# A transformer layer with product-key experts: peer queries in float32, two more gather buffers, the dense sums converted in pairs

## The chip, the core and the metric

The kernel runs on one NeuronCore of one Trainium2 chip. The core has TensorE for matrix products (PE in the rows, PEld for its weight loads), VectorE (DVE), ScalarE (ACT), GpSimd (POOL) and SyncE (SP), which only issues transfers. All run their own instruction queues in order and meet through semaphores. Transfers between the chip's memory (HBM), SBUF and back run on 16 DMA engines; SP issues the plain ones, POOL the indirect ones (gathers). The metric is device time of one execution in microseconds, here 2284.3 (median of 3 runs, 2281.31 to 2289.24).

## What is computed

One layer on 256 tokens of width 2048, all in float32: a mixer (block attention and gated linear attention), cross attention to a memory of 256 tokens, and a product-key expert layer (PEER), each followed by a layer norm of ALPHA times the residual plus the result. The change touches the third part:

```python
q = (xt @ w_query).reshape(T, 8, 2, 128)              # 8 heads, 2 halves
s = einsum('thpd,hpnd->thpn', q, sub_keys)            # scores against 128 keys per half
s_top, i_top = top_k(s, 16)
cand = s_top[:, :, 0, :, None] + s_top[:, :, 1, None, :]
best, pos = top_k(cand.reshape(T, 8, 256), 16)        # 16 of 16384 experts per head
expert_idx, gates = ..., softmax(best)
h = gelu(einsum('td,thkd->thk', xc, expert_down[expert_idx]))   # rows of U
out = einsum('thk,thkd->td', gates * h, expert_up[expert_idx])  # rows of V
```

Each token has 128 slots (8 heads of 16), each slot one of 16384 experts, and each expert a row of 2048 floats in U (peer_u) and one in V (peer_v). A layer norm of ALPHA * x + out ends the kernel.

## The kernel before

The 256 tokens are two sets of 128, s = 0 and s = 1; 128 tokens are the 128 partitions of a tile.

**Split matmuls.** A float32 product is made of three faster ones in the type fp32r: an operand is split into a high part (`wh`, rounded by ACT, L151) and a low part (`wl`, the rest, by DVE, L152), and high x high, high x low and low x high are summed. The activations are split likewise: `h2` has its high part in columns 0 to 255 and its low part in columns 256 to 511 of each 128-row piece (L285, L286).

**Queries.** After the second layer norm (`ln_chunk`, four chunks of 512 columns for each token set) the queries of the heads are made: head 0 for token set 0 first (`scores_half`, L593), so that its route and the first gathers can start, with weights `pw` that are split in advance (`early`, and one piece on POOL); then head 1 for both sets (`peer_scores(1, 1)`), head 0 of set 1 (`scores_half` on raw weights), then heads 2 and 3, 4 and 5, 6 and 7 in pairs (`peer_scores(h0, 2)`), whose weights come in 1 MiB pieces through three buffers `wr`. With raw weights (`wl is None`, L206) PE multiplies in float32, once with the high and once with the low part of h2.

**Routes and gathers.** `route(s, h)` is some thirty small DVE instructions that end in `eidx`, the experts' numbers. `gather` (L671) issues on POOL one indirect transfer of 128 rows of 8 KB, 1 MiB, into the next buffer of a ring, and `u_row` (L685) multiplies it with the tokens on DVE and sums (L689, here called a row). The ring has the three buffers `g` of the pool gp, after head 0 of set 0 also the four slots of `gslots`, and for set 1 the three `wr` buffers (`gw`). All 128 slots of set 0 are gathered, of set 1 the first 83 (`KS = (128, 128 - S2)`). The program's order here is that of a scheduler, which moves instructions within its priorities.

**Dense part and last stage.** The sums over V of the slots gathered so far are not made by gathering: weights are written into matrices A[token, expert] (`one_hot`, `weigh_hot`, `build`; for set 0 in `aq0` and `aq1` during the gathers of set 1, for set 1 right after them in `a1` and in a spill in HBM), and `v_dense` (L804) multiplies A with all of V: 128 tiles of 128 experts, each one load of 1 MiB and 24 matmuls of 512 columns. In tile i ACT and DVE make high and low parts `ah`, `al` of the two 128 x 128 pieces of A (L820, L821; the elements lie 16 apart) and `wh`, `wl` of the tile of V. From here on the order is that of the code. Between the tiles `tick` runs a list of events (`deferred`): the other 45 slots of set 1 as rows of U, then as rows of V, which are added on DVE to `acc` (L697), ALPHA times the tokens of set 1. The events come at an even pace, 96 of them over 124 tiles; a row is gathered two events before DVE takes it. `finish` adds the sums of PE to the residuals and makes the last layer norm.

Of the kernel before, what the change touches and what calls it, by code (L numbers as in the profile page):

```python
# [16 lines left out]
P = 128  # L17
# [21 lines left out]
S2 = 45  # L39
# [17 lines left out]
class Body:  # L57
# [106 lines left out]
    def raw_tiles(self, w, c0):  # L164
        for g in range(4):
            yield g == 0, g == 3, g * 4, self.wload(w, c0, g), None
# [25 lines left out]
    def peer_q(self, xhl, tiles, dst, nc_):  # L192
        ps = [None] * (nc_ // T)
        for first, last, k0, wh, wl in tiles:
            for j in range(nc_ // P):
# [71 lines left out]
    def ln_chunk(self, y, stats, gb, dst, h, c):  # L267
# [15 lines left out]
        H = dst[:, 4 * c:4 * c + 4, h * P:(h + 1) * P]  # L283
        L = dst[:, 4 * c:4 * c + 4, T + h * P:T + (h + 1) * P]
# [285 lines left out]
    def pw_tiles(self, h, early=None, pool=()):  # L570
        for g in range(4):
            raw = self.pw[:, g * 4:(g + 1) * 4, h * T:(h + 1) * T]
            if g == 0 and early:
                wh, wl = early
            else:
                wh, wl = self.wsplit(raw, self.nc.gpsimd if g in pool else self.nc.vector)
            yield g == 0, g == 3, g * 4, wh, wl

    def pw_raw(self, h):
        for g in range(4):  # L580
            yield g == 0, g == 3, g * 4, self.pw[:, g * 4:(g + 1) * 4, h * T:(h + 1) * T], None
# [12 lines left out]
    def scores_half(self, s, h2, tiles):  # L594
        nc, ps = self.nc, self.bank()
        hs = slice(s * P, (s + 1) * P)
        for first, last, k0, wh, wl in tiles:
            n = wh.shape[1]
            for k in range(n):
# [256 lines left out]
    def run(self):  # L856
# [26 lines left out]
        with tc.tile_pool(name="smR", bufs=2) as self.sm:  # L883
# [13 lines left out]
            for c in range(4):  # L897
                self.ln_chunk(y, stats[0], gb, h2, 0, c)
# [128 lines left out]
```

## Time and profile before

| | |
|---|---|
| median of 3 runs | 2284.3 us |
| the profiled execution's own time | 2284.81 us |
| its span, first to last instruction | 2283.1 us |
| PE, PEld busy | 1830.5 us (80%), 1532.5 us (67%) |
| DVE, ACT, POOL busy | 1734.1 us (76%), 938.1 us (41%), 499.8 us (22%) |
| moved by DMA | 629.18 MB, mean 276 GB/s |

Busy shares over the whole span mix stages with different limits, so they are read by window: the stretch of a stage, the busy time of each engine in it, and the share of the 16 DMA engines (a little above 1 when all are full). In such a row the busy times stand in the order PE, PEld, DVE, ACT, POOL. Matmuls are pipelined, so that the mean of one is longer than the distance from one to the next.

### The profile page before, as it was taken

The page shows a single profiled execution, that of the slowest core. Times are in us where ns is not written, and L with a number is a line of the kernel's source. Part 1 is how long each engine was busy: PE and PEld are TensorE (multiplying, and loading weights), DVE is VectorE, ACT ScalarE, POOL GpSimd, SP SyncE. Part 2 cuts the span into 40 slices and gives each one's busy share as a digit, 9 for nine tenths or more (in the row PEclk, how much of TensorE's full clock was granted, in tenths as well). Part 3 has the DMA queues.
Part 4 walks back from the last instruction along what each step waited for, and adds up shares of the span by engine and source line. Part 5 has one row for each costly group of instructions (what it writes and reads, how often), then busy time and mean ns, then how long its engine had stood idle before and what let it go on. Part 6 is the DMA issues. An engine that isn't in the chain of part 4 may idle for free.

```text
span 2283.1 us, 24101 instructions
## 1 busy us (share of the span) xinstructions
PE 1830.5 (80%) x8702; PEld 1532.5 (67%) x8702; DVE 1734.1 (76%) x2517; ACT 938.1 (41%) x1546; POOL 499.8 (22%) x341
## 2 busy tenths in 40 slices
PE   8999999899999969994000550059999999999995
PEld 7778887788888858884000440047888888888884
DVE  5455556644444568899999999998888787888886
ACT  4554544444444441111210650056555555555553
POOL 0000000100000024766437337820111111111111
PEclk9999999999999989997555555579999999999998
DMA  7544557465546628999989999967889898999982
GB/s 229 173 161 155 163 181 276 139 193 186 198 134 221 228 89 329 412 422 379 344 301 364 338 311 347 394 240 270 332 339 347 323 366 314 357 360 330 342 346 92
DMA packets 159639, 629.18 MB, mean 276 GB/s; under 512 B 12176, under 2 KB 24592, under 8 KB 103840
## 3 DMA queue, kind: packets, MB, share of 16 engines
q1 hardware_dynamic: 116176, 312.01, 38.7%
q0 software_dynamic: 43344, 315.64, 36.7%
q8 instruction: 68, 1.11, 0.2%
q14 instruction: 51, 0.42, 0.0%
HBM read 620.27 MB, written 7.34 MB: 275 GB/s over the span
## 4 chain that ended last, share of the span: by engine, by line
PE 64%; DVE 23%; issue 5%; POOL 3%; DMA 3%; ACT 1%; ACTq 0%; SPq 0%; DVEq 0%; POOLq 0%
PE pp L183 9%; PE pp L831 6%; PE pp L830 6%; DVE g L689 6%; PE pp L833 6%; PE pp L224 5%; PE pp L225 5%; PE pp L223 5%; PE pp L185 5%; DVE gslots L689 5%; PE pa L830 4%; PE pa L831 4%; PE pa L833 4%; DVE oh L760 3%; DVE gw L689 2%
## 5 line engine op out<-in xcount | busy, mean ns | idle before, releaser
L152 DVE TENSOR_TENSOR wl<-wr,wh 128x1024 fp32r<-128x1024 f32 x512 | 627.9, 1228 | 418.5 <-ACT wh L151 418.2
L151 ACT CAST wh<-wr 128x1024 fp32r<-128x1024 f32 x512 | 538.4, 1052 | 556.4 <-PE pa L833 213.9
L689 DVE SCALAR_TENSOR_TENSOR g<-g,y 128x2048 f32<-128x2048 f32 x151 | 349.2, 2320 | 20.5 <-DMA g<-in_peer_u_dram,eidx 20.5
L680 POOL DMA_INDIRECT g<-in_peer_u_dram,eidx x151 | 232.9, 1542 | 494.3 <-DVE g L689 385.5
L830 PE MATMUL pp<-wh,ah 128*128 128x512 f32 x640 | 252.0, 394 | 2.3 <-issue 2.3
L831 PE MATMUL pp<-wl,ah 128*128 128x512 f32 x640 | 251.2, 392 | 0.9 <-DVE wl L152 0.7
L833 PE MATMUL pp<-wh,al 128*128 128x512 f32 x640 | 208.6, 391 | 0.0
L207 PE MATMUL pp<-h,wr 128*128 128x256 f32 x768 | 166.6, 379 | 0.0
L207 PEld LDWEIGHTS pp<-h,wr 128*128 128x128 f32 x768 | 145.7, 190 | 19.5
L830 PE MATMUL pa<-wh,ah 128*128 128x512 f32 x384 | 150.8, 393 | 0.0
L831 PE MATMUL pa<-wl,ah 128*128 128x512 f32 x384 | 150.4, 392 | 0.0
L689 DVE SCALAR_TENSOR_TENSOR gslots<-gslots,y 128x2048 f32<-128x2048 f32 x64 | 145.2, 2281 | 6.3 <-DMA gslots<-in_peer_u_dram,eidx 6.3
L736 PE MATMUL pa<-ident,w 128*128 128x128 f32 x2 | 0.9, 460 | 180.4 <-DVE w L705 180.4
L831 PEld LDWEIGHTS pp<-wl,ah 128*128 128x128 f32 x640 | 120.7, 189 | 28.5 <-DVE wl L152 2.6
L830 PEld LDWEIGHTS pp<-wh,ah 128*128 128x128 f32 x640 | 120.5, 188 | 27.9 <-issue 2.5
L833 PEld LDWEIGHTS pp<-wh,al 128*128 128x128 f32 x640 | 120.5, 188 | 27.3
L183 PE MATMUL pp<-x,wh 128*128 128x512 f32 x384 | 136.4, 398 | 0.0
L833 PE MATMUL pa<-wh,al 128*128 128x512 f32 x384 | 129.4, 391 | 0.0
L680 POOL DMA_INDIRECT gslots<-in_peer_u_dram,eidx x64 | 105.9, 1654 | 78.4 <-DVE gslots L689 46.7
L736 PEld LDWEIGHTS pa<-ident,w 128*128 128x128 f32 x2 | 0.4, 182 | 181.1 <-DVE w L705 166.2
L736 PE MATMUL pa<-ident,ij 128*128 128x128 f32 x4 | 1.3, 434 | 147.0 <-DVE ij L661 147.0
L820 ACT CAST ah<-aq 128x128 fp32r<-128x128 f32 x208 | 86.1, 414 | 73.6 <-PE pa L831 73.6
(310 smaller groups left out, 3759.2 us busy)
## 6 DMA issues: line engine op xcount, KB each, us to landing
wr<-in_peer_v_dram SPq DMA_DIRECT2D x128, 1024.0 KB, 6.4
wr<-in_w_in_dram SPq DMA_DIRECT2D x48, 1024.0 KB, 5.1
wr<-in_xattn_wkv_dram SPq DMA_DIRECT2D x32, 1024.0 KB, 5.2
wr<-in_w_out_dram SPq DMA_DIRECT2D x16, 1024.0 KB, 5.3
wr<-in_xattn_wq_dram SPq DMA_DIRECT2D x16, 1024.0 KB, 5.0
wr<-in_xattn_wo_dram SPq DMA_DIRECT2D x16, 1024.0 KB, 5.0
wr<-in_peer_wq_dram SPq DMA_DIRECT2D x12, 1024.0 KB, 15.7
spill<-stg SPq DMA_DIRECT2D x16, 320.0 KB, 2.8
```

Of the source, the lines that this page charges most:

```text
L151: self.nc.scalar.copy(wh, raw)
L152: (eng or self.nc.vector).tensor_tensor(wl, raw, wh.bitcast(F32), op=ALU.subtract)
L183: nc.tensor.matmul(ps[j], wh[:, k, c], xhl[:, k0 + k, :], start=(first and k == 0), stop=False, skip_group_check=True)
L185: nc.tensor.matmul(ps[j][:, :T], wl[:, k, c], xhl[:, k0 + k, 0:T], start=False, stop=(last and k == WK - 1), skip_group_check=True)
L207: self.nc.tensor.matmul(out, wh[:, k, c], x, start=start and i == 0, stop=stop and i == 1, skip_group_check=True)
L223: nc.tensor.matmul(ps[h], xh, wh[:, k, :], start=(first and k == 0), stop=False)
L224: nc.tensor.matmul(ps[h], xh, wl[:, k, :], start=False, stop=False)
L680: self.nc.gpsimd.indirect_dma_start(out=g, out_offset=None, in_=table, in_offset=bass.IndirectOffsetOnAxis(ap=self.eidx[:, s, i:i + 1], ax ...
L689: self.nc.vector.scalar_tensor_tensor(g, g, 1.0, self.h2n[:, s, :], op0=ALU.mult, op1=ALU.mult, accum_out=self.z[:, s, i:i + 1])
L830: nc.tensor.matmul(o, ah[th], wh[:, c, :], start=first, stop=False)
L831: nc.tensor.matmul(o, ah[th], wl[:, c, :], start=False, stop=False)
L833: nc.tensor.matmul(out[th][cp * WK + c], al[th], wh[:, c, :], start=False, stop=last)
```

## The change

Queries: h2 is kept once, unsplit, as the first half of a tile `h2s`, and all queries are float32 matmuls with raw weights, one where there were three of fp32r or two of float32. The splits of `pw` on ACT, DVE and POOL and the low half of h2 go. The other half of `h2s` is two slots of the gather ring: it has 5 buffers for head 0 of set 0 (3 before) and 9 after it (7 before); for set 1 it keeps 6. In the last stage the two pieces of A are converted for two tiles at once (`a_pair`, 256 columns, every second tile), the rows of V of set 1 are added in place to the tokens of set 1 in `h2n` (`acc` goes), which ACT scales by ALPHA after the last row of U, and S2 is 53 in place of 45: 75 slots of set 1 are gathered before the last stage and 53 in it, 114 events over 124 tiles.

```diff
-S2 = 45
+S2 = 53
...
-    def peer_q(self, xhl, tiles, dst, nc_):
+    def peer_q(self, xT, tiles, dst, nc_):
         ps = [None] * (nc_ // T)
-        for first, last, k0, wh, wl in tiles:
+        for first, last, k0, w in tiles:
...
-                out, c = ps[b][:, e * T:(e + 1) * T], slice(j * P, (j + 1) * P)
                 for k in range(4):
-                    start, stop = first and k == 0 and e == 0, last and k == 3
-                    if wl is not None:
-                        self.mm3(out, wh[:, k, c], wl[:, k, c], xhl, k0 + k, start, stop)
-                        continue
-                    for i in range(2):
-                        x = xhl[:, k0 + k, i * T:(i + 1) * T].bitcast(F32)
-                        self.nc.tensor.matmul(out, wh[:, k, c], x, start=start and i == 0, stop=stop and i == 1,
-                                              skip_group_check=True)
+                    self.nc.tensor.matmul(ps[b][:, e * T:(e + 1) * T], w[:, k, j * P:(j + 1) * P], xT[:, k0 + k, :],
+                                          start=first and k == 0 and e == 0, stop=last and k == 3,
+                                          skip_group_check=True)
...
-    def ln_chunk(self, y, stats, gb, dst, h, c):
+    def ln_chunk(self, y, stats, gb, dst, h, c, split=True):
...
+        if not split:
+            nc.scalar.copy(H, src)
+            return
...
-        for first, last, k0, wh, wl in tiles:
-            n = wh.shape[1]
-            for k in range(n):
-                xh, xl = h2[:, k0 + k, hs], h2[:, k0 + k, T + s * P:T + (s + 1) * P]
-                if wl is None:
-                    ops = [(xh.bitcast(F32), wh), (xl.bitcast(F32), wh)]
-                else:
-                    ops = [(xh, wh), (xh, wl), (xl, wh)]
-                for i, (x, w) in enumerate(ops):
-                    nc.tensor.matmul(ps[:, :T], x, w[:, k, :], start=first and k == 0 and i == 0,
-                                     stop=last and k == n - 1 and i == len(ops) - 1)
+        for first, last, k0, w in tiles:
+            for k in range(4):
+                nc.tensor.matmul(ps[:, :T], h2[:, k0 + k, s * P:(s + 1) * P], w[:, k, :], start=first and k == 0,
+                                 stop=last and k == 3)
...
         def add():
-            self.nc.vector.scalar_tensor_tensor(self.acc, g, self.w[:, s, i:i + 1], self.acc,
-                                                op0=ALU.mult, op1=ALU.add)
+            acc = self.h2n[:, s, :]
+            self.nc.vector.scalar_tensor_tensor(acc, g, self.w[:, s, i:i + 1], acc, op0=ALU.mult, op1=ALU.add)
...
+    def residual(self):
+        self.nc.scalar.activation(self.h2n[:, 1, :], self.h2n[:, 1, :], AF.Copy, scale=ALPHA)
...
+        ev.append(lambda: pend.append(self.residual))
         ev += [lambda i=i: row(self.v_row, i) for i in range(KS[1], SLOTS)]
...
+    def a_pair(self, n, r):
+        nc, ah, al = self.nc, [], []
+        for s in range(2):
+            src = self.a_slab(s, n)[:, :, r:r + 2].rearrange("p t i -> p i t")
+            ah.append(self.v.tile([P, 2, P], F32R, name=self.name("ah"), tag="ah", bufs=4))
+            al.append(self.v.tile([P, 2, P], F32R, name=self.name("al"), tag="al", bufs=4))
+            nc.scalar.copy(ah[s], src)
+            nc.vector.tensor_tensor(al[s], src, ah[s].bitcast(F32), op=ALU.subtract)
+        return ah, al
...
-            if i == 2:
-                nc.scalar.activation(self.acc, self.h2n[:, 1, :], AF.Copy, scale=ALPHA)
...
+            if i % 2 == 0:
+                ah2, al2 = self.a_pair(n, r)
+            ah, al = [t[:, i % 2, :] for t in ah2], [t[:, i % 2, :] for t in al2]
...
-            early = self.gp.tile([P, 2, 4, T], F32R, name="early", tag="g")
-            early = self.wsplit(self.pw[:, 0:4, 0:T], None, (early[:, 0], early[:, 1]))
...
-            h2 = self.hl_tile("h2")
+            h2s = self.hlp.tile([P, 4, D], F32, name="h2s", tag="hl")
+            h2 = h2s[:, 0:2, :].rearrange("p a (k t) -> p (a k) t", t=T)
...
-            self.slots = []
+            spare = [lambda k=k: h2s[:, k, :] for k in (2, 3)]
+            self.slots = spare
             self.gather_u(0, (0,))
-            self.slots = [lambda k=k: gs[:, k, :] for k in range(4)]
+            self.slots = spare + [lambda k=k: gs[:, k, :] for k in range(4)]
```

On DVE, between the indices of head 0 (eidx) and the first rows, the kernel before has these (pa is a transposed chunk of the tokens, g a gather buffer, y the tokens):

```order
L286 TENSOR_TENSOR h_6342<-pa_6519,h_6342 128x4x128
L152 TENSOR_TENSOR wl_6557<-pw,wh_6556 128x1024
L286 TENSOR_TENSOR h_6342<-pa_6529,h_6342 128x4x128
L286 TENSOR_TENSOR h_6342<-pa_6538,h_6342 128x4x128
L286 TENSOR_TENSOR h_6342<-pa_6548,h_6342 128x4x128
L152 TENSOR_TENSOR wl_6586<-pw,wh_6585 128x1024
L152 TENSOR_TENSOR wl_6614<-pw,wh_6613 128x1024
L152 TENSOR_TENSOR wl_6642<-pw,wh_6641 128x1024
L689 SCALAR_TENSOR_TENSOR g_6769,z<-g_6769,y 128x2048
L689 SCALAR_TENSOR_TENSOR g_6772,z<-g_6772,y 128x2048
L689 SCALAR_TENSOR_TENSOR g_6775,z<-g_6775,y 128x2048
L689 SCALAR_TENSOR_TENSOR g_6778,z<-g_6778,y 128x2048
```
and the changed kernel these, up to the first instruction of head 1's route (MAX):

```order
L271 TENSOR_TENSOR y<-y,ln_0_5733 128x512
L268 SCALAR_TENSOR_TENSOR y<-y,rr_6352,ln_1_5734 128x512
L669 SCALAR_TENSOR_TENSOR h2s,z<-h2s,y 128x2048 x2
L669 SCALAR_TENSOR_TENSOR g_6622,z<-g_6622,y 128x2048
L669 SCALAR_TENSOR_TENSOR g_6625,z<-g_6625,y 128x2048
L669 SCALAR_TENSOR_TENSOR g_6628,z<-g_6628,y 128x2048
L607 MAX val_6545<-sc_6538 128x8 x2
```
The four residuals of h2 and the four low parts wl are gone, and five rows stand where four stood.

On DVE, further on, between the indices of head 1 and the first MAX of head 2's route, the kernel before has 16 rows, of which these are the last 13 (w is the weights of head 0):

```order
L689 SCALAR_TENSOR_TENSOR g_6808,z<-g_6808,y 128x2048
L689 SCALAR_TENSOR_TENSOR g_6811,z<-g_6811,y 128x2048
L689 SCALAR_TENSOR_TENSOR g_6814,z<-g_6814,y 128x2048
L689 SCALAR_TENSOR_TENSOR gslots,z<-gslots,y 128x2048
L705 TENSOR_TENSOR w<-w,gate 128x16
L689 SCALAR_TENSOR_TENSOR gslots,z<-gslots,y 128x2048
L689 SCALAR_TENSOR_TENSOR g_7070,z<-g_7070,y 128x2048
L689 SCALAR_TENSOR_TENSOR g_7073,z<-g_7073,y 128x2048
L689 SCALAR_TENSOR_TENSOR g_7076,z<-g_7076,y 128x2048
L689 SCALAR_TENSOR_TENSOR gslots,z<-gslots,y 128x2048 x4
L689 SCALAR_TENSOR_TENSOR g_7087,z<-g_7087,y 128x2048
L627 MAX val_6980<-sc_6963 128x8 x2
```
and the changed kernel, from the indices on:

```order
L642 SCALAR_TENSOR_TENSOR eidx<-ij 128x16
L669 SCALAR_TENSOR_TENSOR g_6648,z<-g_6648,y 128x2048
L669 SCALAR_TENSOR_TENSOR g_6651,z<-g_6651,y 128x2048
L669 SCALAR_TENSOR_TENSOR g_6654,z<-g_6654,y 128x2048
L669 SCALAR_TENSOR_TENSOR h2s,z<-h2s,y 128x2048
L669 SCALAR_TENSOR_TENSOR g_6844,z<-g_6844,y 128x2048
L685 TENSOR_TENSOR w<-w,gate 128x16
L607 MAX val_6758<-sc_6741 128x8 x2
```
The route of head 2 stands behind 5 rows where it stood behind 16.

On DVE in the last stage the first three tiles of the kernel before read:

```order
L821 TENSOR_TENSOR al_9576<-aq_7941,ah_9575 128x128
L821 TENSOR_TENSOR al_9580<-a_9039,ah_9579 128x128
L152 TENSOR_TENSOR wl_9586<-wr_9021,wh_9585 128x1024
L152 TENSOR_TENSOR wl_9590<-wr_9021,wh_9589 128x1024
L821 TENSOR_TENSOR al_9621<-aq_7941,ah_9620 128x128
L821 TENSOR_TENSOR al_9625<-a_9039,ah_9624 128x128
L152 TENSOR_TENSOR wl_9631<-wr_9541,wh_9630 128x1024
L152 TENSOR_TENSOR wl_9635<-wr_9541,wh_9634 128x1024
L689 SCALAR_TENSOR_TENSOR g_9461,z<-g_9461,y 128x2048
L821 TENSOR_TENSOR al_9666<-aq_7941,ah_9665 128x128
L821 TENSOR_TENSOR al_9670<-a_9039,ah_9669 128x128
```
and two tiles and the start of the next of the changed kernel, a few tiles further on:

```order
L794 TENSOR_TENSOR al_9553<-aq_7581,ah_9552 128x256
L794 TENSOR_TENSOR al_9557<-a_8652,ah_9556 128x256
L152 TENSOR_TENSOR wl_9563<-wr_9478,wh_9562 128x1024
L152 TENSOR_TENSOR wl_9567<-wr_9478,wh_9566 128x1024
L669 SCALAR_TENSOR_TENSOR g_9513,z<-g_9513,y 128x2048
L152 TENSOR_TENSOR wl_9600<-wr_9515,wh_9599 128x1024
L152 TENSOR_TENSOR wl_9604<-wr_9515,wh_9603 128x1024
L669 SCALAR_TENSOR_TENSOR g_9550,z<-g_9550,y 128x2048
L794 TENSOR_TENSOR al_9635<-aq_7581,ah_9634 128x256
L794 TENSOR_TENSOR al_9639<-a_8652,ah_9638 128x256
```
The two al stand ahead of every second tile's wl, and are twice as wide.

## Rows read from the trace of the kernel before

**Rows 1.** page, part 2: busy tenths in 40 slices
```profile
DVE  5455556644444568899999999998888787888886
```
**Rows 2.** windows: length, busy (x) by engine, granted clock, DMA share, GB/s
```profile
846.00:860.00 14.00, 11.10 (x71) 9.96 (x72) 14.00 (x15) 3.40 (x5) 7.01 (x5) 0.73 0.57 201
860.00:900.00 40.00, 38.20 (x203) 33.96 (x203) 34.91 (x59) 4.54 (x12) 18.04 (x13) 1.00 0.80 291
900.00:1000.00 100.00, 100.00 (x480) 88.54 (x479) 84.72 (x131) 10.35 (x26) 75.98 (x35) 1.00 1.02 417
1000.00:1400.00 400.00, 123.50 (x517) 105.56 (x515) 399.25 (x775) 112.44 (x314) 183.23 (x134) 0.57 0.93 344
1400.00:1505.00 105.00, 0.66 (x2) 0.31 (x2) 93.67 (x91) 3.13 (x11) 90.24 (x40) 0.50 0.98 388
1505.00:1553.00 48.00, 38.02 (x258) 34.70 (x258) 44.94 (x150) 39.46 (x119) 0.41 (x1) 0.92 0.47 147
1553.00:2255.00 702.00, 701.06 (x3054) 574.35 (x3054) 582.45 (x648) 365.05 (x514) 98.83 (x87) 1.00 0.88 330
```
**Rows 3.** chain of waits, 812 to 862 us: start, us, what
```profile
819.51 1.12 DVE wl L152
...
821.24 1.61 DVE nmr L264
...
829.57 5.64 PE pp L606 x46
...
858.65 2.30 DVE g L689 x2
...
861.21 7.27 DMA g<-in_peer_u_dram,eidx
```
**Rows 4.** timelines, POOL and DVE: start, us, instruction, idle before
```profile
846.82 1.33 POOL L680 DMA_INDIRECT g<-in_peer_u_dram,eidx  x1 [18.90 <-DVE y L273]
...
868.58 2.29 DVE L689 SCALAR_TENSOR_TENSOR g<-g,y 128x2048 f32<-128x2048 f32 x1 [3.09 <-DMA g<-in_peer_u_dram,eidx]
```
**Rows 5.** groups by form, DVE, 850 to 1505 us: busy, mean, idle
```profile
L645 DVE TENSOR_TENSOR cand<-val 128x256 f32<-128x256 f32 x15 | 6.0, 403 | 0.0
L152 DVE TENSOR_TENSOR wl<-pw,wh 128x1024 fp32r<-128x1024 f32 x4 | 5.2, 1336 | 0.0
...
L286 DVE TENSOR_TENSOR h<-pa,h 128x512 fp32r<-128x512 f32 x4 | 2.6, 678 | 0.0
```
**Rows 6.** groups by form, DVE, 1400 to 1505 us
```profile
L689 DVE SCALAR_TENSOR_TENSOR g<-g,y 128x2048 f32<-128x2048 f32 x20 | 47.5, 2382 | 6.7 <-DMA g<-in_peer_u_dram,eidx 6.7
L689 DVE SCALAR_TENSOR_TENSOR gw<-gw,y 128x2048 f32<-128x2048 f32 x19 | 44.4, 2334 | 3.7 <-DMA gw<-in_peer_u_dram,eidx 2.8
```
**Rows 7.** groups by form, PE, 850 to 1505 us
```profile
L207 PE MATMUL pp<-h,wr 128*128 128x256 f32 x768 | 166.6, 379 | 0.0
```
**Rows 8.** timeline, ACT: score copies of two pairs of heads
```profile
938.38 1.72 ACT L592 COPY sc<-pa 128x256 f32<-128x256 f32 x4
...
995.47 1.72 ACT L592 COPY sc<-pa 128x256 f32<-128x256 f32 x4
```
**Rows 9.** tile wr, 850 to 1062 us: its loads, queue to landing
```profile
DMA to landing us min/median/max: 6.0/15.8/17.3
```
**Rows 10.** groups by form, DVE, 1580 to 2240 us
```profile
L697 DVE SCALAR_TENSOR_TENSOR acc<-g,w,acc 128x2048 f32<-128x2048 f32 x45 | 105.6, 2346 | 0.0
...
L821 DVE TENSOR_TENSOR al<-aq,ah 128x128 fp32r<-128x128 f32 x198 | 69.1, 373 | 4.7 <-ACT ah L820 2.4 <-PE pa L833 2.3
```
**Rows 11.** waits, 1580 to 2240 us: total, times, longest
```profile
PEld pp L831 <- DVE wl L152: 1.5, 3, 0.5
```
**Rows 12.** timelines, DVE and PE, one tile of the last stage
```profile
1915.76 1.22 DVE L152 TENSOR_TENSOR wl<-wr,wh 128x1024 fp32r<-128x1024 f32 x1
...
1918.97 0.39 PE L831 MATMUL pp<-wl,ah 128*128 128x512 f32 x1
```
**Rows 13.** windows of 5.5 us in the last stage
```profile
2199.50:2205.00 5.50, 5.50 (x26) 4.51 (x25) 5.20 (x6) 2.85 (x5) 1.07 (x1) 1.00 1.02 429
```

More of the change, by code (lines that the diff above doesn't have):

```diff
@@ L165, in raw_tiles @@
         for g in range(4):
-            yield g == 0, g == 3, g * 4, self.wload(w, c0, g), None
+            yield g == 0, g == 3, g * 4, self.wload(w, c0, g)
     def mm3(self, out, wh, wl, xhl, kt, first, last):
@@ L568, in prefetch, with pw_tiles @@
                 g * 512:(g + 1) * 512, 0:512].rearrange("(k p) c -> p k c", p=P))
-    def pw_tiles(self, h, early=None, pool=()):
+    def pw_tiles(self, h):
         for g in range(4):
-            raw = self.pw[:, g * 4:(g + 1) * 4, h * T:(h + 1) * T]
-            if g == 0 and early:
-                wh, wl = early
-            else:
[L576 to L581, printed above, removed]
+            yield g == 0, g == 3, g * 4, self.pw[:, g * 4:(g + 1) * 4, h * T:(h + 1) * T]
     def scores(self, s, h, lhs):
@@ L810, in v_dense @@
                 nc.sync.dma_start(self.a_slab(1, n + NB - 1)[:, t, :], self.spill[:, n - 1, t, :])
-            if i == 2:
-                nc.scalar.activation(self.acc, self.h2n[:, 1, :], AF.Copy, scale=ALPHA)
             if i == NK - 10:
                 self.ln3_vectors()
-            ah, al = [None] * 2, [None] * 2
-            for s in range(2):
-                src = self.a_slab(s, n)[:, :, r]
-                ah[s] = self.v.tile([P, P], F32R, name=self.name("ah"), tag="ah", bufs=4)
-                al[s] = self.v.tile([P, P], F32R, name=self.name("al"), tag="al", bufs=4)
-                nc.scalar.copy(ah[s], src)
-                nc.vector.tensor_tensor(al[s], src, ah[s].bitcast(F32), op=ALU.subtract)
+            if i % 2 == 0:
+                ah2, al2 = self.a_pair(n, r)
+            ah, al = [t[:, i % 2, :] for t in ah2], [t[:, i % 2, :] for t in al2]
             self.load_v(i + WR - 1)
@@ L894, in run @@
             sk = self.sk_transpose(sk, "pp")
-            h2 = self.hl_tile("h2")
+            h2s = self.hlp.tile([P, 4, D], F32, name="h2s", tag="hl")
+            h2 = h2s[:, 0:2, :].rearrange("p a (k t) -> p (a k) t", t=T)
             stats = [self.ln_finish(st, h) for h in range(2)]
             for c in range(4):
-                self.ln_chunk(y, stats[0], gb, h2, 0, c)
-            scored = self.scores_half(0, h2, self.pw_tiles(0, early, (3,)))
+                self.ln_chunk(y, stats[0], gb, h2, 0, c, split=False)
+            scored = self.scores_half(0, h2, self.pw_tiles(0))
             self.table(AF.Exp)
@@ L949, in run @@
             self.total_ticks = HB * WA + (NK - VE) * WV
-            self.acc = self.v.tile([P, D], F32, name="acc")
             self.a1 = self.v.tile([P, NB, P, IB], F32, name="a1")
@@ L967, in finish @@
         st = self.tiny.tile([P, 2, 4, 6], F32, name="st3", tag="bnst", bufs=2)
-        acc, mv, r, nmr = (self.h2n[:, 0, :], self.acc), [None] * 2, [None] * 2, [None] * 2
+        acc, mv, r, nmr = (self.h2n[:, 0, :], self.h2n[:, 1, :]), [None] * 2, [None] * 2, [None] * 2
         def chunk(h, c, engines):
```

6 lines of the change are left out of this document (2 added, 4 removed).

## The prediction

> **What bounds the kernel now.** I read the page's slices first, then the windows cut at the stages, then the chain of waits and the groups inside each window. In the slices VectorE (DVE) is at 8 to 9 tenths from the middle of the run to its end [rows 1]; the windows split that into stages with different limits (their busy columns are PE, PEld, DVE, ACT, POOL) [rows 2].
>
> From 846 to 1505 us lies the gather stage: 211 gathers of U, each 1 MiB, each followed by one dot product on DVE. DVE is busy 399.25 of the 400 us from 1000 to 1400: there it is the bound, with the DMA engines at 0.93. Before that it isn't: from 860 to 900 it works 34.91 of 40 us, from 900 to 1000 84.72 of 100, and the DMA engines are at 0.80 and 1.02 [rows 2]. So 5.1 + 15.3 = 20.4 us of DVE time are lost at the front. From 1400 to 1505 DVE works 93.67 of 105 us at 388 GB/s, and its idle time ends on gathers [rows 2, 6]: a tail of plain rows, bound by DMA.
>
> From 1553 to 2255 us lies the last stage, the 128 dense tiles of V. PE is busy 701.06 of 702 us, so it is the bound; DVE has 582.45 us of work there and the queues move 330 GB/s [rows 2]. The weight load waited for DVE 1.5 us in all, 3 times [rows 11]. Work put on DVE or the DMA engines here is free as long as the low part wl arrives before its matmul. In a tile with a row it is ready at 1915.76 + 1.22 = 1916.98 and used at 1918.97: 2.0 us of room [rows 12].
>
> **The change, part by part.** The sums go against the profiled execution (2284.8 us, span 2283.1); the median of the runs shown is 2284.3, so half a microsecond separates them.
>
> *Up to the first eidx.* The low part of a weight tile goes from DVE (1.12 us on the chain) [rows 3], and POOL's piece of the same split with it; behind it nmr, which writes one number per partition, took 1.61 us [rows 3], and I put 1.5 of that on the POOL op that ran beside it (an estimate; nothing else on DVE grew there). Together -2.6. The 46 matmuls that took 5.64 us [rows 3] become 14 behind the last transpose, in float32. Their price: 480 records fill 100 us of PE [rows 2], and each float32 matmul leaves two (768 records [rows 7] for 3 x 128 matmuls), so 0.417 us each and 5.8 for 14: no gain and no loss. PE has stood idle before them, and after such a pause its granted clock is 0.73 over 846 to 860 [rows 2]; wholly at the half level the 14 take 11.7, +6. Value -2.6, between -5 and +3.5.
>
> *From eidx to the first rows.* Four low parts (5.2 us) and four residuals of h2 (2.6 us) leave DVE [rows 5]: -7.8. They stand between eidx and the first row, where DVE never idles (14.00 of 14.00) [rows 2]. What is late next is the first gather: POOL issues it at 846.82 [rows 4], a gather took 7.27 us on the chain [rows 3], so no row can run before 854.1 where one now starts at 858.65 [rows 3]. DVE is ready 7.8 earlier, at 850.9, and waits 3.2. I keep -7.8 here and put that wait into the next term.
>
> *Idle of DVE at the front.* Five slots in place of three let gathers 4 and 5 go without waiting for a row; now row 4 waits 3.09 for its data [rows 4]. Then the scores: a pair of heads follows the one before by 995.47 - 938.38 = 57.1 us [rows 8], 53.3 of it float32 matmuls (256 records at 0.208). Half of these go, which leaves 30.4. Four loads of weights per pair through three buffers with 15.8 us to landing [rows 9] give (15.8 + 6.7) / 3 = 7.5 each, 30 a pair, so loads and matmuls are level. I put the scores of heads 2, 4 and 6 at some 907, 941 and 973, where now they stand at 938, 995 and 57 later. Routing is then there to fill DVE while gathers are late, and after head 1's indices the order has 5 rows ahead of it, not 16. Of the 20.4 I leave 12: 3 for the first gather, some 6 for rows 2 to 5 at the DMA pace, 3 for the first scores. Value -8, between 0 and -17 (all but the first wait).
>
> *Eight rows less.* At DVE's own price 8 x 2.36 = 18.9 [rows 6]; at the tail's pace, 105 us for 39 rows [rows 2, 6], 21.5. They go at the tail, so -20.
>
> *The last stage.* DVE gains 16 row instructions of 2.35 us [rows 10], 37.6 us. An al takes 373 ns for 128 elements [rows 10], now one of 256 replaces two. Nothing shows it; two of the old are 746, a contiguous one of 256 takes 403 [rows 5]. The row nearest in form is the strided al itself, so I take its slope above the fixed part: 403 ns for 256 contiguous elements against 678 for 512 [rows 5] is 1.07 ns an element over 128 fixed; (373 - 128) / 128 = 1.9 ns; 128 + 256 x 1.9 = 620. So 128 x 0.126 = 16 us are saved, and DVE stands at 582 + 22 = 604 of 702. By the contiguous row DVE would have 28 us less still; as PE is the bound, the sum stays. In tiles that make a pair DVE does up to 0.75 us more ahead of wl, out of 2.0 us of room; where two rows fall in one tile (four times, three before) PE may wait some tenths each. DMA: 16 MiB more, (330 x 702 us = 231.7 MB) + 16.8 = 248.4 MB, 354 GB/s, where 5.5 us windows reach 429 [rows 13]. The copy of the residual on ACT moves from tile 2 to the middle, into ACT's idle half. Value +1, between 0 and +6.
>
> Sum: -2.6 - 7.8 - 8 - 20 + 1 = -37.4, so 2284.8 - 37.4 = **2247.4**.
>
> **Rivals.** *The front is bound by bytes.* DMA is at 1.02 from 900 to 1000 [rows 2], and the weight loads come sooner, into the gathers. Then neither the shorter DVE list nor the earlier scores move the end, and only the tail and the first scores count: 2284.8 - 2.6 - 20 + 1 = 2263. For it: 417 GB/s there. Against: 860 to 900 runs at 291 GB/s [rows 2], 40 x 0.126 = 5 MB of room, five rows, which five slots can use. 0.2.
>
> *The last stage becomes bound by DMA* (the other side). A row that is late holds the wl queued behind it on DVE, and PE waits. The stage needs 248.4 MB; if the mix could give no more than the 330 GB/s it moved [rows 2], it would take 753 us, +51, and the total is 2298. It turns slower than before once the stage's rate falls under 248.4 MB / (702 + 37) us = 336 GB/s. For it: share 0.88 already. Against: 417 GB/s over 100 us, and 429 in this very stage [rows 2, 13]. 0.04 for slower, and 0.04 for a stage that gives the gain back and no more. The Trainium skill ("SBUF — State Buffer", section "Summary: rules for kernel authors") has transfers from HBM estimated at about 358 GB/s. By that figure the 2 MiB of a tile with a row need an estimated 5.86 us where a tile has 5.48, and a stage without slack would come out up to 40 us longer, at an estimated 2287; the windows at 417 and 429 [rows 2, 13] say that it is no ceiling on this core.
>
> *DVE in the last stage.* With al at 746 and two rows in a tile, PE waits up to 1.5 us four times, +6: 2252. It stays inside the forecast's range.
>
> *The spare slots don't serve*, because the gathers into h2's tile wait for the matmuls that read it. Then the first rows wait for the scores of head 1 and more, +30 on the front: 2277. Against: the matmuls read the first two quarters of that tile, the gathers fill the other two. 0.02.
>
> **How the numbers follow.** The forecast has 0.70, the byte-bound front 0.2, the dead slots 0.02, a last stage bound by DMA 0.04 near the old time and 0.04 slower. Ends: all terms at their low ends, -5 - 7.8 - 17 - 21.5 = 2234; at their high ends, the first wait not hidden, +3.5 - 4.6 - 18.9 + 6 = 2271. Range 2235 to 2266: it holds the forecast and the first rival, and leaves 0.15 to 0.2 out. Under 0.3% (7 us) this measurement tells nothing apart; the first three cases lie beyond it: faster 0.92, same 0.04, slower 0.04.
>
> **What would show it.** Right: score copies 57 apart now some 30 apart; first row within 4 us of its gather's landing and no L152 ahead of it; DVE from 860 to 1000 above 0.92 busy; a gather stage from eidx to the last gathered row of some 623 us, not 659; a last stage of 702 to 705 us with PE above 0.99 and windows of 350 GB/s; al of 256 at 0.5 to 0.7 us. Wrong: PE waiting for wl in the last stage by more than 6 us, or a front where DVE's idle of 20 us stays with the DMA engines at 1.0.

## The result, and the profile after

The changed kernel takes 2261.8 us (median of 4 runs, 2258.2 to 2266.6), the kernel before in the same session 2284.4: 22.6 us less. The ratio of the runs is 0.9892 (95% interval 0.9878 to 0.9907; the quotient of the two medians, 0.9901, lies in it). The profiled execution of the changed kernel is its fastest run, 2258.2 us with a span of 2256.5, and stands 26.6 us under the profiled one of before.

Cut at four points (the end of the first `eidx`, the end of the last gathered row, the start of the first dense matmul, the end of the last one), the two traces compare so, in us:

| stretch | before | changed | difference | put at |
|---|---|---|---|---|
| up to the first eidx | 845.9 | 844.1 | -1.8 | -2.6 |
| eidx to the last gathered row | 658.7 | 629.6 | -29.1 | -35.8 |
| to the first dense matmul | 48.0 | 48.9 | +0.9 | } |
| the dense tiles | 706.9 | 709.6 | +2.7 | } +1 |
| the last layer norm | 23.6 | 24.3 | +0.7 | } |

These are the four instructions in the timelines of the changed kernel (start, length, instruction):

```profile
843.95 0.18 DVE L642 SCALAR_TENSOR_TENSOR eidx<-ij 128x16 int32<-128x16 f32 x1
...
1471.45 2.29 DVE L669 SCALAR_TENSOR_TENSOR g<-g,y 128x2048 f32<-128x2048 f32 x1 [1.76 <-DMA g<-in_peer_u_dram,eidx]
...
1522.63 0.47 PE L818 MATMUL pp<-wh,ah 128*128 128x512 f32 x1 [2.77 <-issue]
...
2231.61 0.62 PE L821 MATMUL pa<-wh,al 128*128 128x512 f32 x2
```

The largest miss is the gather stage, 6.7 us longer than forecast; the stretches behind it are 3.3 us longer, the first one 0.8. The windows by stage (columns as in [rows 2]) say where the gather stage lost it:

```profile
846.00:860.00 14.00, 13.13 (x59) 11.23 (x60) 9.13 (x9) 2.30 (x4) 11.06 (x9) 0.82 0.75 270
860.00:900.00 40.00, 38.10 (x184) 33.20 (x183) 36.78 (x60) 3.66 (x12) 15.56 (x12) 1.00 1.01 406
900.00:1000.00 100.00, 71.87 (x319) 60.90 (x317) 85.92 (x194) 17.36 (x44) 45.05 (x33) 0.87 0.99 407
1000.00:1400.00 400.00, 68.66 (x259) 57.83 (x259) 399.30 (x719) 104.59 (x296) 188.96 (x136) 0.50 0.93 339
1550.00:2230.00 680.00, 677.26 (x2955) 554.56 (x2954) 581.81 (x528) 328.69 (x373) 143.30 (x100) 1.00 0.92 352
```

Against [rows 2]: VectorE has less to do right after the indices (9.13 us of 14, where it was full), and from 860 to 900 the DMA engines are now full. But from 900 to 1000 VectorE is still idle 14.1 us. Over 846 to 1000 its idle time is 154 - 131.8 = 22.2 us, where it was 20.4 and should have come to 12. In the kernel before, that idle time was waits on gathers (waits of VectorE from 846 to 1000 us: total, times, longest):

```profile
DVE g L689 <- DMA g<-in_peer_u_dram,eidx: 13.7, 11, 5.1
DVE gslots L689 <- DMA gslots<-in_peer_u_dram,eidx: 6.3, 9, 1.4
```

The same waits in the changed kernel name a piece that the prediction does not have:

```profile
DVE gr L649 <- ACT gate L647: 10.6, 1, 10.6
DVE g L669 <- DMA g<-in_peer_u_dram,eidx: 6.8, 4, 3.5
DVE h2s L669 <- DMA h2s<-in_peer_u_dram,eidx: 4.5, 2, 2.8
```

The gather waits are 11.3 us. The rest is one stall of 10.6 us in which VectorE waits for no gather at all, but for a tiny instruction of ScalarE in a route. The timeline of VectorE around it (start, length, instruction, idle time before it and what ended that):

```profile
977.27 0.41 DVE L613 FIND_INDEX8 pos<-best,mr 128x8 uint32<-128x256 f32 x1
988.28 0.16 DVE L649 RECIPROCAL gr<-gs 128x1 f32<-128x1 f32 x1 [10.61 <-ACT gate L647]
```

that of ScalarE:

```profile
982.29 0.59 ACT L204 COPY pq<-pp 128x512 f32<-128x512 f32 x1 [19.88 <-PE pp L200]
982.78 0.22 ACT L634 CAST idf<-idx 128x32 f32<-128x32 uint32 x1
985.75 0.59 ACT L204 COPY pq<-pp 128x512 f32<-128x512 f32 x1 [2.75 <-PE pp L200]
986.23 1.72 ACT L580 COPY sc<-pa 128x256 f32<-128x256 f32 x4
987.85 0.31 ACT L647 ACTIVATE gate<-best,gm 128x16 f32<-128x16 f32 x1
```

and that of TensorE:

```profile
978.54 7.17 PE L200 MATMUL pp<-h2s,wr 128*128 128x256 f32 x32 [2.64 <-DMA wr<-in_peer_wq_dram]
```

Read them from the last one: TensorE starts the last weight tile of heads 6 and 7 when it lands, at 978.5. ScalarE, in order, has been standing at the copy of those queries (`pq`) for 19.9 us. Behind that copy in its queue stands `gate`, whose input VectorE had written at 975, and for `gate` waits the reciprocal on VectorE, behind which stand rows that then run without a wait. In the chain of waits (start, us, what) the tile is the longest piece:

```profile
950.44 28.05 DMA wr<-in_peer_wq_dram
```

28 us for 1 MiB, where the loads of the kernel before landed after 6 to 17.3 us [rows 9].

### The profile page after: what moved, and what is told of

It is laid out like the page before. It is cut to its first block, busy times and chain, and to the rows that moved or that the text cites. A ratio compares the mean times of both kernels' runs of the same rounds, so it can differ in the third digit from the quotient of the medians.

```text
span 2256.5 us, 22663 instructions
## 1 busy us (share of the span) xinstructions
PE 1748.3 (77%) x8238; PEld 1454.3 (64%) x8238; DVE 1717.4 (76%) x2382; ACT 905.0 (40%) x1408; POOL 493.4 (22%) x348
## 3 DMA queue, kind: packets, MB, share of 16 engines
q8 instruction: 64, 1.05, 0.2%
## 4 chain that ended last, share of the span: by engine, by line
PE 68%; DVE 20%; DMA 6%; issue 4%; POOL 2%; ACT 1%; SPq 0%; ACTq 0%; DVEq 0%; POOLq 0%
PE pp L183 9%; PE pp L819 6%; PE pp L821 6%; PE pp L818 6%; PE pp L218 6%; PE pp L219 6%; PE pp L217 5%; PE pp L185 5%; DVE g L669 5%; PE pa L821 4%; PE pa L819 4%; PE pa L818 4%; DMA wr<-in_peer_wq_dram 3%; DVE oh L744 3%; DVE gslots L669 3%
## 5 line engine op out<-in xcount | busy, mean ns | idle before, releaser
L669 DVE SCALAR_TENSOR_TENSOR g<-g,y 128x2048 f32<-128x2048 f32 x138 | 316.6, 2304 | 12.2 <-DMA g<-in_peer_u_dram,eidx 12.2
L660 POOL DMA_INDIRECT g<-in_peer_u_dram,eidx x138 | 208.9, 1514 | 425.7 <-DVE g L669 343.6
L660 POOL DMA_INDIRECT g<-in_peer_v_dram,eidx x53 | 72.7, 1372 | 263.9 <-DVE y L678 235.0
L678 DVE SCALAR_TENSOR_TENSOR y<-g,w,y 128x2048 f32<-128x2048 f32 x53 | 124.4, 2347 | 0.0
L669 DVE SCALAR_TENSOR_TENSOR gslots<-gslots,y 128x2048 f32<-128x2048 f32 x48 | 109.7, 2301 | 0.0
L185 PE MATMUL pp<-x,wl 128*128 128x256 f32 x384 | 108.5, 283 | 0.0
L200 PE MATMUL pp<-h2s,wr 128*128 128x256 f32 x384 | 92.0, 401 | 17.6 <-DMA wr<-in_peer_wq_dram 17.6
```

Source lines behind the costliest of these rows:

```text
L185: nc.tensor.matmul(ps[j][:, :T], wl[:, k, c], xhl[:, k0 + k, 0:T], start=False, stop=(last and k == WK - 1), skip_group_check=True)
L660: self.nc.gpsimd.indirect_dma_start(out=g, out_offset=None, in_=table, in_offset=bass.IndirectOffsetOnAxis(ap=self.eidx[:, s, i:i + 1], ax ...
L669: self.nc.vector.scalar_tensor_tensor(g, g, 1.0, self.h2n[:, s, :], op0=ALU.mult, op1=ALU.mult, accum_out=self.z[:, s, i:i + 1])
L678: self.nc.vector.scalar_tensor_tensor(acc, g, self.w[:, s, i:i + 1], acc, op0=ALU.mult, op1=ALU.add)
```

## The experiments

Each was run beside the kernel before, on one chip and in one session; the ratio is to that.

| run | median, us | ratio | 95% interval |
|---|---|---|---|
| changed kernel | 2261.8 | 0.9892 | 0.9878 to 0.9907 |
| e1 copies behind | 2255.1 | 0.9870 | 0.9850 to 0.9891 |
| e2 no late weights | 2248.7 | 0.9839 | 0.9820 to 0.9859 |
| e3 45 slots | 2280.8 | 0.9988 | 0.9973 to 1.0002 |
| e4 old queries | 2269.3 | 0.9934 | 0.9917 to 0.9951 |
| e5 e1 with late vectors | 2249.3 | 0.9847 | 0.9833 to 0.9860 |
| e6 e5 with 61 slots | 2231.4 | 0.9770 | 0.9757 to 0.9783 |
| e7 no spare slots | 2267.1 | 0.9921 | 0.9908 to 0.9934 |
| e8 single pieces | 2256.9 | 0.9880 | 0.9865 to 0.9895 |
| e9 e5 with 65 slots | 2228.2 | 0.9755 | 0.9740 to 0.9770 |
| e10 e5 with 69 slots | 2244.1 | 0.9816 | 0.9802 to 0.9830 |
| e11 e6 with an early tile | 2229.0 | 0.9750 | 0.9736 to 0.9764 |
| e12 changed, late vectors | 2261.6 | 0.9898 | 0.9883 to 0.9913 |

**e1: is the stall a matter of order?** `gated` and `cast` are the last scaling of the gate and the cast `abf` of the route before; only ScalarE's order changes.

```diff
-                self.peer_scores(h0, 2, h2)
+                if h0 == 6:
+                    with tc.issue_after(self.gated.ins), tc.issue_after(self.cast.ins):
+                        self.peer_scores(h0, 2, h2)
+                else:
+                    self.peer_scores(h0, 2, h2)
```

> The changed kernel (2261.8 us), with one thing moved: on ScalarE the copies of the queries of heads 6 and 7 (pq, and the score copies behind them) stand behind the cast abf, the two gate instructions and the cast idf of head 5's route, and no longer ahead of them. Nothing else is reordered on any engine. In the trace of the changed kernel VectorE stands still for 10.6 us at 977.7, waiting for that gate, which stands behind the copies, which wait for TensorE, which waits for a weight tile that landed 28 us after its issue. Theory 'order': the stall is one of queues in order, and the expected gain at the front was lost in it; without it 2250 to 2254, VectorE's idle time from 846 to 1000 us falls from 22 to 12 us or less. Rival 'bytes': the DMA engines are full at the front (0.99 at 407 GB/s), the rows of those 10 us are owed to them in any case; then the idle time turns up before the next rows as waits on gathers, and the time is 2259 to 2263.

In e1 the window of 900 to 1000 us, and the waits of VectorE from 846 to 1530 us:

```profile
900.00:1000.00 100.00, 70.74 (x316) 59.98 (x314) 93.77 (x212) 17.05 (x44) 46.68 (x35) 0.86 1.02 424
```
```profile
DVE g L669 <- DMA g<-in_peer_u_dram,eidx: 10.0, 13, 3.4
DVE h2s L669 <- DMA h2s<-in_peer_u_dram,eidx: 4.6, 2, 3.1
DVE val L607 <- ACT sc L580: 4.6, 2, 3.9
```

The wait for `gate` is gone, VectorE works 93.8 us of the 100 (85.9), the queues move 424 GB/s (407). A wait of 3.9 us for the scores themselves takes a part of its place; the gather waits did not grow. From eidx to the last row it is 620.9 us (629.6). That speaks for the theory "order"; the rival "bytes" would have had the idle time come back as gather waits. It is less than the theory expected: the idle time from 846 to 1000 us fell from 22.2 to 14.6 us, not to 12, and the median of 2255.1 lies between the two ranges. The gather stage is 8.7 us shorter, the median 6.8; in the profiled execution of e1 the dense tiles took 715.3 us where they took 709.6, and e5 takes that up.

**e2: the weights out of the way.**

```diff
-        tiles = self.pw_tiles(h0) if nh == 1 else self.raw_tiles(self.A["peer_wq"][0], h0 * T)
+        tiles = self.pw_tiles(h0) if nh == 1 else ((g == 0, g == 3, g * 4, self.pw[:, g * 4:(g + 1) * 4, :])
+                                                   for g in range(4))
```

> The changed kernel, in which the queries of heads 2 to 7 are made with the weights of heads 0 and 1 that are in SBUF already, so the 12 loads of 1 MiB (9 of them after the first indices) go and with them every wait for them; the queries of heads 2 to 7, their experts and the output are other than the reference's. Both theories expect the stall of 10.6 us and the wait of 3.5 us for the first scores to go. 'Order': that is all, 14 us, about 2248. 'Bytes': the 9.4 MB that go are 23 us of the DMA engines at 407 GB/s, so the waits of the first five rows (7.8 us in all) shrink too and the tail, bound by DMA, comes sooner; 2238 to 2244. If it stays above 2256, neither holds and VectorE's own list sets the front.

2248.7 us, what "order" expected, though the 9.4 MB would be 23 us of full queues. VectorE is idle 8.0 us from 846 to 1000 (14.6 in e1), gather stage 614.5 us. So the loads themselves, without the stall, cost the front about 6 us: bytes have a part in the front, the smaller one.

**e12, e5: the vectors of the last layer norm.** In both the loads go from tile 118 to tile 124:

```diff
-            if i == NK - 10:
+            if i == NK - 4:
```

> The kernel of the first experiment (copies of heads 6 and 7 behind the gate; 2255.1 us, gather stage 620.9 us, dense tiles 715.3 us) with the loads of the last layer norm's two vectors (2 MiB) issued at tile 124 of 128, behind the last row, and no longer at tile 118. In that kernel's trace the DMA engines are full from 2160 to 2180 us (424 to 429 GB/s), a tile of V lands late, TensorE waits 2.4 + 0.5 us and then runs 10 us at a clock of 0.66. Theory: that stall and its half clock are 5 us that the last stage pays for the 16 more rows and the vectors meeting; without it dense tiles of 709 to 711 us and 2249 to 2252. Rival: the tile is late because of the rows alone; then 2254 to 2256 and a stall at the same place. Rival on the other side: the vectors come too late for the layer norm, 2256 or more.

> The changed kernel (2261.8 us median of 2258.2 to 2266.6; its profiled execution, 2258.2, lost only 0.6 us where the vectors load) with those loads at tile 124 and nothing else. In three other runs with 53 slots and the loads at tile 118 TensorE waited 1.2 to 2.9 us there and twice ran some 10 us at part of the clock; dense tiles took 713 to 715 us. Theory: the changed kernel pays the same in most executions, and the gap of 3.6 us between its median and its profiled execution is that stall; without it the median falls to 2256 to 2259 with dense tiles of 709 to 711 us. Rival: the gap lies elsewhere in the run; 2260 to 2263.

In e1 a tile of V meets the vectors; TensorE's timeline there, and the windows:

```profile
2180.49 0.76 PE L818 MATMUL pp<-wh,ah 128*128 128x512 f32 x1 [2.37 <-ACT wh L151]
2181.75 0.80 PE L819 MATMUL pp<-wl,ah 128*128 128x512 f32 x1 [0.50 <-DVE wl L152]
```
```profile
2170.00:2180.00 10.00, 8.12 (x36) 6.34 (x34) 4.71 (x5) 2.68 (x4) 2.01 (x2) 1.00 1.01 424
2180.00:2190.00 10.00, 9.01 (x26) 6.82 (x27) 7.92 (x6) 4.64 (x7) 0.00 (x0) 0.66 0.70 281
```

Full queues, a late tile, 2.9 us of waiting, then 26 matmuls in 10 us where 45 are usual: the granted clock was 0.66, so that a part of the stretch ran at the lower level (1.2 GHz). In e5 the stall is gone, the dense tiles take 709.8 us (715.3) and the median is 5.8 us lower. On the changed kernel itself (e12) nothing is gained: the theory was wrong, the rival right. Why the same edit is worth 5.8 us in one kernel and nothing in the other stays open. The gap between the changed kernel's median and its profiled execution may lie in the stall of the front (not shown: there is one trace of that kernel); in e12's execution that stall was longer:

```profile
DVE gr L649 <- ACT gate L647: 16.8, 1, 16.8
```

(e12, waits of VectorE from 846 to 1490 us), with a gather stage of 633.1 us. The same wait is 10.6 us in the profile of the changed kernel, 12.7 in e3, 14.6 in e7, 10.7 in e8; the changed kernel was profiled with the shortest. Between e12 and e5, which differ by ScalarE's order alone, lie 12.3 us by their medians, and 11.1 us of gather stage in their traces; between the changed kernel and e1, by the same edit, 6.8 and 8.7. So the order costs some 7 to 12 us in the median.

**e3, e4: each half of the change alone.** e3 is the changed kernel with `S2 = 45`; e4 is the kernel before with these edits of the change:

```diff
-S2 = 45
+S2 = 53
...
+            if i % 2 == 0:
+                ah2, al2 = self.a_pair(n, r)
...
+            acc = self.h2n[:, s, :]
```

> The changed kernel with 45 slots of set 1 in the last stage in place of 53, all else as it is. It measures the terms 'eight rows less' and 'the last stage' together. By the prediction's terms (-20 and +1) it comes at 2281; by the two traces, in which the stretch from the last gathered row to the end grew by 4.3 us and a row costs 2.36 (VectorE's price) to 2.7 us (the tail's pace), at 2276 to 2279. Rival: the last stage already pays for the 16 more rows by contention on the DMA engines; then 2266 to 2272.

> The kernel before (2284.4 us) with the other half of the change alone: 53 slots in the last stage, A converted in pairs, the rows of V added in place; queries, splits and gather buffers as before. By the two traces the query part gave 1.8 us up to the first indices, took 7.8 us of work from VectorE and gave none of it back in idle time (22 us at the front, before and after), so that this half is worth 16 to 19 us: 2265 to 2269. By the prediction's terms (-20 + 1): 2265, and the changed kernel should then stand 18 us under it, where it stands some 5. Rival: the query part gave all that was expected (18 us) and the last stage gave it back; then 2278 to 2282.

e3 came at the time that the prediction's terms give, e4 just past the upper end of the traces' 2265 to 2269: this half gives 14.3 us alone, where its terms had 19. In e4's trace the gather stage is 21.7 us shorter (637.0) and the dense tiles 6.3 us longer (713.2). With the rows of before, the gather stage of e3 is 650.7 us, 8.0 under before: that is the 7.8 us of work taken off VectorE and nothing for its idle time. From e3 to the changed kernel it falls by 21.1, of which 2.1 is the shorter stall. Alone the halves give 2.8 and 14.3 us against 22.6 together; the difference of 5.5 us is not taken apart by any run (the stall of 12.7 us in e3 and the longer dense tiles in e4 are in the traces).

**e7: without the two buffers.**

```diff
-            self.slots = spare
+            self.slots = []
...
-            self.slots = spare + [lambda k=k: gs[:, k, :] for k in range(4)]
+            self.slots = [lambda k=k: gs[:, k, :] for k in range(4)]
```

> The changed kernel (2261.8 us) without the two gather buffers in h2s: 3 buffers for head 0 of set 0 and 7 after it, as in the kernel before. Theory 'buffers feed VectorE', as the prediction had it: the fourth and fifth gather wait for a row again, VectorE idles some 3 to 6 us more at the front; 2264 to 2268. Rival 'buffers delay the weights': two gathers fewer stand ahead of each weight tile, which lands nearer to the 16 us of the kernel before than to 20; the stall of 10.6 us shrinks and the time is 2254 to 2260.

The time is that of the first theory, by another way: the fifth row ends as early as with five buffers (868.4 and 868.8 us). Later in the front the waits on gathers are 3.4 us longer (14.7 against 11.3 up to 1000 us) and the stall 4.0 (14.6). The rival is refuted: the weights land later still, 24.6 us in the median (19.9).

**e8: single pieces of A.** `v_dense` of the kernel before, two instructions of 128 columns per tile on each engine.

```diff
-            if i % 2 == 0:
-                ah2, al2 = self.a_pair(n, r)
-            ah, al = [t[:, i % 2, :] for t in ah2], [t[:, i % 2, :] for t in al2]
+            for s in range(2):
+                src = self.a_slab(s, n)[:, :, r]
...
+                nc.scalar.copy(ah[s], src)
+                nc.vector.tensor_tensor(al[s], src, ah[s].bitcast(F32), op=ALU.subtract)
```

> The changed kernel (2261.8 us) with the pieces of A converted one tile at a time, as in the kernel before (128 columns, four small instructions per two tiles and engine). VectorE gets 128 x (0.373 - 0.298) x 2 = 19 us more work in the last stage (0.373 us for 128 columns in the kernel before, 0.595 for 256 in the changed one) and stays under 610 of 707 us. Theory: TensorE is the bound, the pairs bring nothing by themselves: 2260 to 2264. Rival: with 53 rows more than the old slack of 2.0 us is used up in tiles with a row, TensorE waits some tenths in many of them; 2268 to 2275. Rival on the other side: the wider pieces are what makes TensorE wait for the low part; 2256 to 2259.

Dense tiles 710.5 us (709.6); VectorE has 13 us more to do in them (577.6 of 655 us from 1560 to 2215, 564.6 in the changed kernel). The pairs bring nothing that shows, as TensorE is the bound. They may even cost something: 2256.9 us is in the range of the second rival (2256 to 2259) and not of the theory, and all four runs (2256.7 to 2257.7) lie under all four of the changed kernel, though the intervals of the ratios overlap. In the traces TensorE waits for `wl` and `wh` in the dense tiles 1.9 us in all, in the changed kernel 3.5, and the dense tiles are no shorter for it; this stays open.

**e6, e9, e10: how far do the slots go?** e5 with more slots of set 1 left to the last stage.

```diff
-S2 = 53
+S2 = 61    # e9: 65, e10: 69
```

> The kernel of the experiment before, with 61 slots of set 1 in the last stage. TensorE bounds that stage, VectorE has 582 of 680 us there and the queues 352 GB/s. Theory: room is left for eight more slots: the gather stage loses 8 rows (19 to 21 us), VectorE gets 37.6 us more in the last stage (some 620 of 680) and the queues 376 GB/s, and the stage grows by no more than 4 us: 15 to 19 us under the experiment before, 2232 to 2236. Rival: the last stage turns bound by its transfers; with 16.8 MB more at 352 GB/s it grows by 48 us, and the time is 2270 to 2280; a part of it, 2245 to 2255, if late tiles bring half clock several times.

> The kernel with 61 slots in the last stage (2231.4 us; VectorE 140 of 150 us busy and the DMA engines at 0.99 from 1850 to 2150 us, dense tiles 710.9 us) with 65. Theory 'still room': four rows less in the gather stage, 9.5 to 11 us, and dense tiles of 711 to 714: 2221 to 2225. Rival 'full': the DMA engines have nothing left between 1850 and 2150, so the 8.4 MB more (20 us at 420 GB/s) come as late rows that hold the low parts behind them; 2228 to 2240.

> The same with 69 slots. VectorE would have some 150 of 150 us in that stretch, the queues 415 GB/s. Theory 'still room': 2211 to 2216. Rival 'full': two rows in a tile are later than the 2.0 us of room again and again, TensorE waits and runs at half clock behind each wait; 2230 to 2260.

The window of 1850 to 2000 us with 61, 65 and 69 slots, one line each:

```profile
1850.00:2000.00 150.00, 150.00 (x657) 122.81 (x656) 139.99 (x110) 74.08 (x84) 42.12 (x28) 1.00 0.99 398
```
```profile
1850.00:2000.00 150.00, 148.41 (x644) 120.06 (x643) 143.14 (x112) 69.95 (x79) 49.35 (x30) 1.00 0.99 400
```
```profile
1850.00:2000.00 150.00, 143.95 (x613) 116.40 (x612) 140.38 (x108) 66.98 (x76) 57.64 (x31) 0.98 0.98 393
```

and what TensorE waited for in the dense tiles with 69:

```profile
PE pp L819 <- DVE wl L152: 24.8, 19, 3.5
```

VectorE, in turn, waited there for rows of V (and 7.9 us for rows of U):

```profile
DVE y L678 <- DMA g<-in_peer_v_dram,eidx: 15.3, 13, 2.8
```

At 61 the room is real (dense tiles 710.9 us), and the time came just under the range expected. At 65 and 69 it came in the ranges of the rival "full". At 65 dense tiles take 718.1 us, and the four rows gain 3 us, within the error. At 69 they take 744.3: rows come late and hold the low parts behind them. That is the prediction's rival of a last stage bound by DMA; it decides from some 400 GB/s on, and the changed kernel needs 352. VectorE is busy 140 to 143 of the 150 us in all three, so it has little room left there either.

**e11: one weight tile before the gathers.**

```diff
+            self.early = h2s[:, 3, :].rearrange("p (k c) -> p k c", c=512)
+            nc.sync.dma_start(self.early, A["peer_wq"][0][1536:2048, 512:1024].rearrange("(k p) c -> p k c", p=P))
...
-            self.slots = spare
+            self.slots = spare[:1]
```

> The kernel with 61 slots (2231.4 us) in which one of the weight tiles of heads 2 and 3 is loaded into one of the two spare gather buffers of h2s before the gathers begin, where the DMA engines are at 0.15 (810 to 846 us), and that buffer joins the ring only after head 0; so 1 MiB leaves the full front, each later weight tile is asked for one buffer earlier, and four buffers serve head 0. Theory 'the front now waits for weights': the scores of heads 2, 4 and 6 (now at 902, 938, 986) come some 8 to 10 us earlier each, the waits of 3.5 us for the first and 4.0 us for the last scores go: 2224 to 2228. Rival 'the front is bound by bytes': 1 MiB is 2.5 us, less what the missing buffer costs: 2229 to 2234.

2229.0 us, at the edge of the rival's range; the profiled execution was no faster than e6's, the scores came at 906, 940 and 986 (902, 938 and 986 in e6), and the gather stage took 598.8 us (597.6). Nothing is shown for it. e9 and e11 are the fastest versions, 2.4 to 2.5% under the kernel before.

## Why the prediction was right, and its size not

Right in direction, and near in four of five terms. The measured 2261.8 us lies in the stated range of 2235 to 2266, but nearer to the first rival (2263) than to the forecast (2247.4), and neither of the two mechanisms is what happened: the range was wide enough to hold both, and that is luck. Of the 14.4 us between forecast and median, 10.8 show in the trace of the profiled execution; the other 3.6 lie between that execution, which was the fastest, and the median.

*Up to the first eidx* (-2.6): -1.8. *From eidx to the first rows* (-7.8): came in full: in e3, which keeps the old 45 slots, the gather stage is 8.0 us shorter and the idle time at the front no shorter. *Eight rows less* (-20): 21.1, or 19.0 without the change in the stall. *The last stage* (+1, to +6): +4.3. The piece that was put at tenths is a place where the last `weigh` of set 1 stands on ScalarE: it waits 5.7 us for a row, `ah` and `wh` stand behind it, and TensorE waits 0.9 + 0.8 us (ScalarE's timeline in the changed kernel):

```profile
1876.14 0.21 ACT L684 ACTIVATE w<-z 128x5 f32<-128x5 f32 x1 [5.71 <-DVE g L669]
1876.26 1.19 ACT L793 CAST ah<-aq 128x256 fp32r<-128x256 f32 x2
```

This is not the price of the eight slots: with 45 slots the same `weigh` waits 5.7 us in e3, in the kernel before it waited 0.2 (waits of ScalarE in e3, then the timeline of the kernel before):

```profile
ACT w L684 <- DVE g L669: 5.7, 1, 5.7
```
```profile
1900.63 0.21 ACT L704 ACTIVATE w<-z 128x13 f32<-128x13 f32 x1 [0.22 <-DVE g L689]
```

By the code it comes with the new event `residual`: that event stands in the list behind the last `weigh`, so that the next row runs the last two rows of U and this `weigh` in one tile, where the kernel before leaves the `weigh` to the next event. No run moved the event.

The al of 256 columns was put at 620 ns and takes 595 (mean of 98).

*Idle of DVE at the front* (-8): this is the step that failed; it came out at +1.8. Its first two parts were near (put at 9, the gather waits of the first five rows were 7.8 us; put at 3, one wait of 3.5 us stands ahead of head 2's route, though the trace puts it on a gather of head 1 and not on the scores). Its third, that routing would fill VectorE because "loads and matmuls are level", rested on the landing of 15.8 us that the old kernel shows [rows 9]. There TensorE took 13.3 us for a tile; now it takes 7.2 to 9.9 and asks for the next one sooner, while the DMA engines are full from 860 on, not from 900. (From 860 to 880, ahead of the first of these loads, that is the two more gather buffers: 1.01 in the changed kernel, 0.84 in e7 without them.) The score copies were put at 907, 941 and 973 and came at 903.7, 941.7 and 986.2. And the forecast watched TensorE and the queues, not the engine between: ScalarE's in-order queue passed the wait for a late tile to VectorE, which needed nothing of that tile. VectorE was busy 0.88 of the stretch from 860 to 1000 us, where the prediction's sign was more than 0.92; in e1 it is 0.94. Take the order away and the gather stage is 620.9 and 622.0 us (e1, e5), where 623 was forecast, and e5, which moves the vectors too, comes to 2249.3 beside the 2247.4. That is in part a sum of errors: the idle time at the front is still 14.6 us in e1 and 16.5 in e5, not 12.

The Trainium skill ("Perfetto Trace Analysis", section "Tensor Engine Instruction (MATMUL, LD_WEIGHTS)") says that ScalarE, VectorE and GpSimd execute strictly in order while TensorE may reorder a little. This case agrees for ScalarE and VectorE: VectorE stood 10.6 to 16.8 us waiting for a `gate` that was queued on ScalarE behind copies that it has nothing to do with, and the stall went when e1 changed the order.

Of the rivals, the byte-bound front had named 2263, close to the median, with the sign that VectorE's idle time stays while the queues are at 1.0. The sign came, the mechanism for the most part did not: e1 loads the same bytes and the time fell, though e2 shows some 6 us that the weight loads cost. The spare slots serve (e7). The last stage has its DMA bound 8 to 12 slots further out.

What stays open: why the stall varies from 10.6 to 16.8 us between these runs, what the vectors' loads cost the changed kernel, and whether heads 4 and 5 would gain from the same reordering.

## What to carry to other kernels

When a producer becomes faster, follow its result through every engine that passes it on, and ask what stands behind it in that engine's queue and who waits for that; a copy that waits for a transfer does not belong ahead of small steps of another chain. The landing time of a transfer is no constant: take it from a stretch where the queues are as full as they will be. Where TensorE bounds a stage, work can be moved into it until its windows show that the DMA engines, or the engine that takes the work, are full; with 61 slots the DMA engines stood at 0.99 and VectorE at 0.93, and the eight slots on the way there gave another 17.9 us (e5 to e6).

## What the runs showed of the hardware

The DMA queues give a reason for the late weight tiles. From 952 to 968 us in the changed kernel, with two weight loads outstanding beside the gathers for most of it (queue, kind: packets, MB, share; q0 has the gathers, q1 the plain loads):

```profile
q0 software_dynamic: 730, 5.31, 78.7%
q1 hardware_dynamic: 730, 1.43, 23.0%
```

The two queues got the same number of packets, 730 each. A gather's packets average 7.3 KB, those of a weight load (512 columns, 2 KB a row) 2.0 KB, so the loads have a fifth of the bytes: 1.43 MB in 16 us, 89 GB/s, and two loads of 1.05 MB need an estimated 23.6 us of that; the later one landed after 28.1. The kernel before shares its queues in the same way, with nearly equal counts from 928 to 938 us:

```profile
q0 software_dynamic: 458, 3.29, 78.0%
q1 hardware_dynamic: 454, 0.93, 23.8%
```

What differs is how often a tile is asked for. The nine loads behind the first indices in the kernel before and in the changed one (SyncE: start of the first, time to the end of the last issue):

```profile
896.46 114.55 SPq L146 DMA_DIRECT2D wr<-in_peer_wq_dram  x9
```
```profile
880.30 70.51 SPq L146 DMA_DIRECT2D wr<-in_peer_wq_dram  x9
```

That is one per 14.3 us before, an estimated 73 GB/s, and one per 8.8 us now, an estimated 120 GB/s: more than the 89 to 93 GB/s that the loads get beside gathers, so they wait for one another. This is worked out from the counts; no run tests it. The Trainium skill ("DMA: Bandwidth & Descriptors", section "Queues, rings and completion order") says that each DMA engine goes round the queues packet by packet. The equal counts agree with equal turns; how much an engine takes in one turn no run here shows. Weight loads in 8 KB rows might land sooner; that was not tried.

This core moved 398 to 400 GB/s over 150 us in the last stage with 61 and 65 slots, and 424 over the 100 us from 900 on in e1. The 358 GB/s that the prediction quotes from the Trainium skill ("SBUF — State Buffer", section "Summary: rules for kernel authors") is no ceiling here.
